# Two heads' value products as one piece of half-width matmuls, in a decoder layer on one Trainium2 core

## The chip, the core and the metric

The kernel runs on one core of a Trainium2 chip. Its engines run in parallel, each through its own queue in order: TensorE (PE for its matmuls, PEld for the loads of the stationary operand), VectorE (DVE), ScalarE (ACT), GpSimd (POOL) and SyncE (SP, which here issues the DMAs). The metric is the device time of one execution in microseconds (us). An execution that is profiled has a span, from the first to the last instruction, and a time of its own that is a little longer.

## The reference

The input is x, 512 tokens by 1024 channels in float32. After an RMS norm one projection gives queries, keys, values and gates for two mixers.

- Mixer A (MoBA) has 8 heads of 64 channels. With 512 tokens there are two blocks of 256 keys, and top-3 plus the own block selects all of them, so each head is causal attention over 512 keys with a T5 bias that depends on the distance.
- Mixer B (NSA) has 8 heads in two groups of four; a group shares its keys and values. It has three branches: attention to 31 compressed positions, attention to selected blocks (all 8 of them here), and a window of 512 (everything before the query). The selected branch and the window branch are again causal attention over 512 keys, with keys and values of their own. The three are summed with sigmoid gates.

Both outputs y are multiplied by SiLU(z), go through their branch weights, are merged with sigmoid gates, and pass the output projection, whose result is added to x. For this change the core is, for each head:

```
P = softmax(scale * Q K^T + bias, causal)      512 x 512
O = P V                                        512 x 64
y = O * SiLU(z)
```

MoBA has 8 such products, NSA 16 (8 heads by 2 branches), and NSA adds the compressed branch to the same sum.

## The kernel before

**Numbers in two parts.** All matmuls work on operands split into a high and a low part, hi + lo. The projections use a float32 form in three passes (hi·hi, hi·lo, lo·hi). P and V are split into float16 hi and lo.

**Units.** A `Unit` is one attention product: 8 for MoBA, 16 for NSA. For query block b (128 queries, b from 3 down to 0), `Unit.qk` makes the scores of b+1 key blocks in PSUM. `Unit.bias` (DVE, line 1117) adds the bias table T, takes the row minimum and writes a score buffer of the tag "sb" (7 of 3 KB a partition). `Unit.soft` computes exp (ACT, L1128), the gate factor and reciprocal, P's high part (ACT, L1135) and its low part (DVE, L1139), both float16, into the same buffer. `Unit.send` has SP issue one DMA transpose (L243) that writes P's 2(b+1) blocks, turned, into the unit's tile "dst", and the score buffer is free when it has landed. There are two dst tiles; `Unit.start` takes one when there is room.

**Value products.** `Unit.pv(kb)` (L1152) multiplies for key block kb, in the order 0, 3, 2, 1. The stationary operand is the 128 x 128 tile [V_hi | V_lo] of that key block, the moving operand P's turned blocks, 512 - 128 kb columns, first the high and then the low part: 8 matmuls for a unit, with 512, 512, 128, 128, 256, 256, 384 and 384 columns. PSUM tile O (one buffer of one bank) collects V_hi·P in rows 0 to 63 and V_lo·P in rows 64 to 127. A MoBA unit fills O alone; in NSA the two branches of a head add up in one O, and `before` (L1291) adds the compressed branch with one 128 x 128 matmul of 512 columns (`vz`, V of that branch, with rows of the other head set to zero).

**Taking O out.** `o_out` adds the two halves for each of the 16 heads: ACT copies rows 64 to 127 out with a scale (L1179), and DVE computes rows 0 to 63 times the scale plus that copy (L1183) into rows of `ys`, a tile of a pair of heads. When the second head is there and the gate `zs` is ready, `y_try` multiplies y by z (L1193), and ACT and DVE split it into hi and lo (L1194, L1195).

**Order.** The order of all instructions is made when the program is built: a small planner runs streams (`Run`) against planned costs of each engine and of the DMA queue. Stream A issues scores, V the value products, Z takes dst tiles, F the large projections, B and Y prepare; `yield n` gives a piece its planned cost, and a piece is issued when the planner holds its inputs for ready. F fills TensorE while attention waits. F's last part, `branch(1, j)` and the output, needs all y of mixer B. On the chip each engine then runs its list in order, with semaphores.

**Other buffers.** "nxn" is the scratch of the QK norms (two buffers; ACT writes squares at L772, DVE sums them at L773), "a" a pool of 27 tiles of 2 KB, "ge" four small tiles.

Of the kernel before, what the change touches and what calls it, by code (L numbers as in the profile page):

```python
# [12 lines left out]
F32 = mybir.dt.float32  # L13
# [16 lines left out]
C32 = 32  # L30
CMPH = 256
# [10 lines left out]
NATT = 27  # L42
NQK = 6
NSB = 7
NXN = 2
# [61 lines left out]
def hybrid_kernel(ctx: ExitStack, tc: tile.TileContext, x, x0, xT, wtok, wchan, gains, w1,  # L107
# [28 lines left out]
    RES = {"g": (pg, 2), "s": (pss, 2), "t": (pst, 3), "o": (pso, 1), "sb": (sp, NSB), "gmt": (sp, 3), "nraw": (sp, 4),  # L136
# [319 lines left out]
    first = alloc("dst", "x0", (P, 2048))  # L456
# [358 lines left out]
    def proj_norm(name, first=False, tags="gggg"):  # L815
        two = []

        def emit(t, ps):
# [7 lines left out]
            if name == "kb":  # L826
                e_ = sp.tile([P, 24], F32, name=nm("ge"), tag="ge", bufs=4)
                ch.do({"A": 164}, lambda e: e.activation(e_, ps[:, 256:280], AF.Exp, scale=nrx[:, t:t + 1]))
# [173 lines left out]
    def compress_v2(G):  # L1002
# [12 lines left out]
        vt = att("vz").rearrange("p (g i d) -> p g i d", g=2, i=2)  # L1015
# [23 lines left out]
    class Unit:  # L1039


        def __init__(u, q, ks, v, T, gate, first, last, before=None, after=None):
            u.q, u.ks, u.v, u.T, u.gate = q, ks, v, T, gate
            u.first, u.last, u.before, u.after = first, last, before, after
            u.c = {}
            u.st = u.mate = u.dst = None
            u.early = False
            u.todo = []

# [4 lines left out]

        def start(u):
            yield lambda: 0.0 if u.todo else None
            yield room("dst")
            u.dst = alloc("dst", "dst", (P, 2 * NT * S), F16)
            for f in u.todo:
                f()  # L1060

        def send(u, b, z):
# [6 lines left out]
            t = dma_transpose(u.blocks(b * P, n, S), z["pp"], n)  # L1069
# [3 lines left out]
        def blocks(u, o, n, step):  # L1073
            a = u.dst[:, o:o + P]
            return bass.AP(tensor=a.tensor, offset=a.offset, ap=[list(a.ap[0]), [step, n], [1, P]])

        def moving(u, kb, i):
            step = P + i * S
            return u.blocks(kb * step + (i + kb) * S, NT - kb, step)
# [30 lines left out]
        def bias(u, c, b, sps, frees, T, last=False):  # L1110
            z, L, st = {}, P * (b + 1), u.stats()

            def f(e):
                z["t"] = alloc("sb", "sb", (P, 3 * S // 2))
# [6 lines left out]
            c.do({"D": 57 + cd(L)}, f, frees, "sb")  # L1121
# [22 lines left out]
        def pv(u, kb):  # L1144
            yield need(*(("p", id(u), b) for b in range(kb, NT)))
            if kb == 0 and u.first:
                yield room("o")
                O[0] = psum("o", "O")
            n, v = S - kb * P, u.v()[kb]
            out = O[0][:, S - n:].rearrange("p (b q) -> p b q", q=P)  # L1150
            for i in range(2):
                nc.tensor.matmul(out, v, u.moving(kb, i), start=(u.first and kb == i == 0),  # L1152
                                 stop=(u.last and kb == i == 1 and not u.before))
            yield 2 * max(3 + 0.417 * n, 70)
            if kb == 1:
                release(u.dst)
            if kb == 1 and u.last:
                if u.before:
                    yield from u.before(O[0])
                u.after(O[0])  # L1160
# [6 lines left out]
    def o_out(O, m, h):  # L1167
        k = (m, h // 2)
        row = 64 * (h % 2)
        if row == 0:  # L1170
            ys[k] = att("ys", F32)
        y = ys[k]
        ch = Chain(now[0] + 230)
        z = {}
        r = vst[:, int(m == "b"), KT + 3:KT + 4]

        def f(e):
            z["t"] = alloc("gmt", "ot", (DH, S))
            e.activation(z["t"], O[64:128, :], AF.Copy, scale=r[64:128])  # L1179
        ch.do({"A": 571}, f, None, "gmt")  # L1180

        def f(e):
            e.scalar_tensor_tensor(y[row:row + 64, :], O[0:64, :], r[0:64], z["t"], op0=ALU.mult, op1=ALU.add)  # L1183
            release(O, ch.t)
        ch.do({"D": 659}, f, lambda: z["t"])
        if row:
            ch.mark(("ys",) + k).call(lambda: y_try(k))

    def y_try(k):
        if ("ys",) + k in done and ("zs",) + k in done:  # L1190
            y, z, hi, lo = ys[k], zs[k], att("yh"), att("yl")
            ch = Chain(max(done[("ys",) + k], done[("zs",) + k]))
            ch.do(either(512), lambda e: e.tensor_mul(y, y, z))  # L1193
            ch.do({"A": ca(512)}, lambda e: e.copy(hi, y))  # L1194
            ch.do(either(512), lambda e: e.tensor_sub(lo, y, hi.bitcast(F32)))  # L1195
            ch.mark(("y",) + k)
            yhl[k] = hi, lo, ch


    def moba_units():  # L1200
        us = []
        for h in range(8):
# [4 lines left out]
            def pre(h=h, p=p, i=i, box=box):  # L1207
                if i == 0:
# [6 lines left out]
                     lambda h=h: heads("v", h), lambda box=box, i=i: box["T", i], None, True, True, None, lambda o, h=h: o_out(o, "a", h))  # L1215
            us.append((pre, u))
        return us


    def nsa_units(g):  # L1220
# [63 lines left out]
        for i in range(4):  # L1284
            h = 4 * g + i
            for br in range(2):
                def before(o, i=i):
                    yield lambda: 0.0 if len(box["c"]) > i // 2 else None
# [441 lines left out]
```

## Time and profile before

| | |
|---|---|
| time, three runs | 426.15 to 426.85 us, median 426.71 |
| profiled execution | 427.12 us, span 424.9 us, granted clock 1.00 |
| PE busy, PEld busy | 415.7 us (98%), 325.9 us (77%) |
| DVE busy, ACT busy | 366.1 us (86%), 307.3 us (72%) |
| value products (L1152) | 192 matmuls, first at 71.1 us, last at 318.2 us |
| mean share of the DMA queue's packets | 69.7% of 16 engines' span |

A busy PE is not a PE at its peak: matmuls overlap in the pipeline, and a matmul's row shows its latency, not the time until the next may start. How fast PE goes is read from the starts of matmuls that follow one another.

### The profile page before, as it was taken

The page shows a single profiled execution, that of the slowest core. Times are in us where ns is not written, and L with a number is a line of the kernel's source. Part 1 is how long each engine was busy: PE and PEld are TensorE (multiplying, and loading weights), DVE is VectorE, ACT ScalarE, POOL GpSimd, SP SyncE. Part 2 cuts the span into 40 slices and gives each one's busy share as a digit, 9 for nine tenths or more (in the row PEclk, how much of TensorE's full clock was granted, in tenths as well). Part 3 has the DMA queues.
Part 4 walks back from the last instruction along what each step waited for, and adds up shares of the span by engine and source line. Part 5 has one row for each costly group of instructions (what it writes and reads, how often), then busy time and mean ns, then how long its engine had stood idle before and what let it go on. Part 6 is the DMA issues. An engine that isn't in the chain of part 4 may idle for free.

```text
span 424.9 us, 7105 instructions
## 1 busy us (share of the span) xinstructions
PE 415.7 (98%) x2131; PEld 325.9 (77%) x2131; DVE 366.1 (86%) x946; ACT 307.3 (72%) x809; POOL 36.4 (9%) x37
## 2 busy tenths in 40 slices
PE   9999999999998999999999999999999999999996
PEld 8878876778976777987777766666678888888886
DVE  6968779999899898969999998997966876699993
ACT  7997658897799799728999998897953543445620
POOL 0016000125220214000000000000000000000000
PEclk9999999999999999999999999999999999999999
DMA  8961967668989988821879679779878499170233
GB/s 290 298 201 37 184 215 177 131 166 208 261 238 216 196 157 201 225 88 25 165 154 174 169 187 183 166 127 198 150 183 305 144 383 322 43 222 3 61 137 100
DMA packets 116693, 75.30 MB, mean 177 GB/s; under 512 B 89072, under 2 KB 92016, under 8 KB 116656
## 3 DMA queue, kind: packets, MB, share of 16 engines
q1 hardware_dynamic: 116656, 74.86, 69.7%
q8 instruction: 17, 0.28, 0.3%
q14 instruction: 20, 0.16, 0.2%
HBM read 51.11 MB, written 2.75 MB: 127 GB/s over the span
## 4 chain that ended last, share of the span: by engine, by line
PE 55%; ACT 19%; DVE 14%; DMA 5%; issue 5%; SPq 0%; POOL 0%; DVEq 0%; ACTq 0%; POOLq 0%
PE pgc L435 17%; PE pgt L435 12%; PE po L435 9%; PE pbr L435 6%; DMA dst<-sb 5%; PE pgf L697 5%; ACT sb L1128 5%; ACT wh L400 4%; ACT sb L1135 3%; DVE sb L1117 3%; DVE sb L1139 3%; DVE wl L410 2%; PE O L1152 2%; PE sps L1097 1%; ACT vh L400 1%
## 5 line engine op out<-in xcount | busy, mean ns | idle before, releaser
L435 PE MATMUL pgc<-hh,wh 128*128 128x512 f32 x208 | 86.8, 417 | 0.0
L435 PE MATMUL pgc<-hh,wl 128*128 128x512 f32 x208 | 81.5, 392 | 0.0
L435 PE MATMUL pgc<-hl,wh 128*128 128x512 f32 x208 | 81.3, 391 | 0.0
L410 DVE TENSOR_TENSOR wl<-wr,wh 128x512 fp32r<-128x512 f32 (+1 forms) x112 | 73.3, 667 | 9.2 <-ACT wh L400 8.8
L400 ACT CAST wh<-wr 128x512 fp32r<-128x512 f32 (+1 forms) x111 | 64.1, 598 | 8.7 <-DMA wr<-in_wbr 5.2
L1128 ACT ACTIVATE sb<-sb,sst 128x512 f32<-128x512 f32 (+3 forms) x96 | 53.1, 554 | 14.0 <-DVE sst L1117 13.7
L435 PE MATMUL pgt<-wh,hh 128*128 128x512 f32 (+2 forms) x160 | 58.6, 366 | 0.1
L435 PE MATMUL pgt<-wl,hh 128*128 128x512 f32 (+2 forms) x160 | 56.0, 350 | 0.8 <-DVE wl L410 0.8
L435 PE MATMUL pgt<-wh,hl 128*128 128x512 f32 (+2 forms) x160 | 55.9, 349 | 0.0
L1117 DVE CUSTOM_DVE_ANT_0 sb<-sps,T,gst 128x512 f32<-128x512 f32 (+3 forms) x96 | 51.4, 545 | 5.1 <-DMA dst<-sb 3.5
L1139 DVE SCALAR_TENSOR_TENSOR sb<-sb,sst 128x512 f16<-128x512 f32 (+3 forms) x96 | 51.0, 547 | 3.2 <-ACT sb L1135 2.8
L1135 ACT ACTIVATE sb<-sb,sst 128x512 f16<-128x512 f32 (+3 forms) x96 | 50.6, 551 | 3.4 <-DVE sst L1131 3.0
L435 PEld LDWEIGHTS pgc<-hh,wh 128*128 128x128 f32 x208 | 39.2, 188 | 8.6
L435 PEld LDWEIGHTS pgc<-hh,wl 128*128 128x128 f32 x208 | 39.1, 188 | 8.5
L435 PEld LDWEIGHTS pgc<-hl,wh 128*128 128x128 f32 x208 | 39.2, 188 | 6.8
L487 POOL TENSOR_TENSOR nr<-nss,mhalf 128x8 f32<-128x8 f32 (+1 forms) x16 | 30.9, 1937 | 108.1 <-DVE nss L486 80.5
L1097 PE MATMUL sps<-qkt,qkt 128*128 128x384 f16 (+3 forms) x160 | 36.0, 319 | 1.8 <-DVE sst L1117 1.7
L435 PEld LDWEIGHTS pgt<-wl,hh 128*128 128x128 f32 x160 | 30.2, 189 | 5.2 <-DVE wl L410 1.4
L435 PEld LDWEIGHTS pgt<-wh,hh 128*128 128x128 f32 x160 | 30.2, 189 | 4.5 <-DVE X L910 0.4
L435 PEld LDWEIGHTS pgt<-wh,hl 128*128 128x128 f32 x160 | 30.2, 189 | 3.2
L435 PE MATMUL pbr<-yh,wh 128*128 128x512 f32 x64 | 26.5, 414 | 0.0
L1097 PEld LDWEIGHTS <-qkt 128*128 128x128 f16 x160 | 11.1, 98 | 19.2 <-issue 14.4
(229 smaller groups left out, 781.9 us busy)
## 6 DMA issues: line engine op xcount, KB each, us to landing
wr<-in_wchan SPq DMA_DIRECT2D x52, 256.0 KB, 3.4
wr<-in_wtok SPq DMA_DIRECT2D x36, 256.0 KB, 3.8
wq<-in_wout SPq DMA_DIRECT2D x36, 256.0 KB, 4.7
T<-rtab SPq DMA_DIRECT2D x16, 256.0 KB, 4.0
wr<-in_w SPq DMA_DIRECT2D x16, 256.0 KB, 3.2
wr<-in_wbr SPq DMA_DIRECT2D x16, 256.0 KB, 3.5
xr<-in_x SPq DMA_DIRECT2D x8, 256.0 KB, 5.4
x<-in_xT SPq DMA_DIRECT2D x7, 256.0 KB, 5.5
```

What stands on the lines that cost most here:

```text
L400: e.copy(hi, raw)
L410: c.do(either(n), lambda e, hi=hi, lo=lo, raw=raw: e.tensor_sub(lo, raw, hi.bitcast(F32))).mark((w, 1, i))
L435: nc.tensor.matmul(dst, sts[i][a], mvs[i][b], start=(start and i == a == b == 0), stop=(stop and i == n - 1 and (a, b) == passes[-1]), ski ...
L487: c.do({"p": 700 + 150 * w}, lambda e: e.tensor_tensor(v(dst), v(ss), mhalf[:parts, :w], op=ALU.pow))
L697: nc.tensor.matmul(ps[t][:, :n], (hl if a else hh)[:, k, t * P:(t + 1) * P], ws[k][b], start=(k == a == b == 0), stop=(k == KT - 1 and b = ...
L1097: nc.tensor.matmul(sps[:, :n].rearrange("p (t n) -> p t n", n=P), qs, k4[:, x, j, :b + 1], start=not x, stop=bool(x))
L1117: e.tensor_tensor_reduce(z["sb"], sps[:, :L], T[:, S - L:], scale=nrunscale, scalar=3e38, op0=ALU.add, op1=ALU.min, accum_out=st[:, 0, b:b ...
L1128: c.do({"A": 279 + 0.834 * L}, lambda e: e.activation(z["sb"], z["sb"], AF.Exp, bias=st[:, 0, b:b + 1], scale=-1.0, accum_out=st[:, 1, b:b ...
L1135: e.activation(z["pp"][:, :L], z["sb"], AF.Copy, scale=s_)
L1139: c.do({"d": 59 + cd(L)}, lambda e: e.scalar_tensor_tensor(z["pp"][:, L:], z["sb"], s_, z["pp"][:, :L], op0=ALU.mult, op1=ALU.subtract))
L1152: nc.tensor.matmul(out, v, u.moving(kb, i), start=(u.first and kb == i == 0), stop=(u.last and kb == i == 1 and not u.before))
```

## The change

`Pair` takes the value products of two units, in MoBA of two neighbouring heads, in NSA of one branch of two neighbouring heads (two pairs add up in one O). A half-width matmul has a stationary operand of 64 columns, V_hi or V_lo of one unit, and writes 64 rows of O: the first unit rows 0 to 63, the second rows 64 to 127. For each key block there are three products, V_hi·P_hi, V_lo·P_hi and V_hi·P_lo, each for the first and then the second unit: 24 matmuls for a pair, issued as one piece with a planned cost. V_lo·P_lo is left out. All eight parts of P must have landed before the first matmul.

O now holds two heads' finished sums, so `o_out` runs once for a pair: with `zs` ready one DVE operation of 128 x 512 computes O times the scale times z; otherwise ACT copies O with the scale into `ys` and DVE multiplies by z later. The compressed branch takes two 128 x 128 matmuls for a pair of heads (V_hi, V_lo) in place of one for each head.

The dst tile holds 40 blocks of 128 columns (10 KB a partition in place of 8), the second unit's blocks laid between the first's (`row`), so that each transpose writes one unbroken stretch. There are still two dst tiles, now of a pair each. Score buffers become 5 large ("sb", b = 3, 2) and 4 of half the size ("sh", b = 1, 0). To make room, "nxn" has one buffer, the pool "a" 26, "ge" three. The tiles that bring x for the last sum are taken from "dst" one at a time. The order of NSA's units becomes head 0 selected, head 1 selected, head 1 window, head 0 window.

```diff
-NATT = 27
+NATT = 26
-NSB = 7
-NXN = 2
+NSB = 5
+NSH = 4
+NXN = 1
...
-                vz[g], vh[:, g].rearrange("p s d -> p (s d)").bitcast(F32).unsqueeze(1).to_broadcast([P, 2, P]),
-                hmask.unsqueeze(2).to_broadcast([P, 2, P])), vh if g else None)
+                vz[g], vh[:, g].bitcast(F32).unsqueeze(2).to_broadcast([P, 2, 2, DH]),
+                hmask.unsqueeze(1).unsqueeze(3).to_broadcast([P, 2, 2, DH])), vh if g else None)
...
-            t = dma_transpose(u.blocks(b * P, n, S), z["pp"], n)
+            o = u.row(b)
+            t = dma_transpose(u.dst[:, o * P:(o + n) * P].rearrange("p (n q) -> p n q", q=P), z["pp"], n)
...
+        def row(u, b):
+            return 38 - 12 * b if u.side else 10 * b
...
-            z, L, st = {}, P * (b + 1), u.stats()
+            z, L, st, tag = {}, P * (b + 1), u.stats(), "sb" if b > 1 else "sh"
...
-        def pv(u, kb):
-            yield need(*(("p", id(u), b) for b in range(kb, NT)))
...
-            for i in range(2):
-                nc.tensor.matmul(out, v, u.moving(kb, i), start=(u.first and kb == i == 0),
-                                 stop=(u.last and kb == i == 1 and not u.before))
-            yield 2 * max(3 + 0.417 * n, 70)
...
+        def pv(p):
+            yield need(*(("p", id(u), b) for u in p.us for b in range(NT)))
...
+            for kb in (0, 3, 2, 1):
+                n = S - kb * P
+                for vi, pi in ((0, 0), (1, 0), (0, 1)):
+                    for r, u in enumerate(p.us):
+                        out = o[DH * r:DH * r + DH, S - n:].rearrange("p (b q) -> p b q", q=P)
+                        nc.tensor.matmul(out, v[r][kb][:, vi * DH:(vi + 1) * DH], u.moving(kb, pi),
+                                         start=p.first and kb == vi == pi == 0,
+                                         stop=p.last and kb == pi == 1 and not p.before)
+            yield 200 + sum(3 * 0.417 * (S - kb * P) for kb in range(NT))
+            release(p.dst)
...
-        def f(e):
-            z["t"] = alloc("gmt", "ot", (DH, S))
-            e.activation(z["t"], O[64:128, :], AF.Copy, scale=r[64:128])
-        ch.do({"A": 571}, f, None, "gmt")
...
-            e.scalar_tensor_tensor(y[row:row + 64, :], O[0:64, :], r[0:64], z["t"], op0=ALU.mult, op1=ALU.add)
...
+        if ("zs",) + k in done:
+            z = zs[k]
+            ch.t = max(ch.t, done[("zs",) + k])
+            ch.do({"D": 602}, lambda e: e.scalar_tensor_tensor(z, O, r, z, op0=ALU.mult, op1=ALU.mult), O)
+            y_split(k, ch)
+        else:
+            y = ys[k] = att("ys", F32)
+            ch.do({"A": 571}, lambda e: e.activation(y, O, AF.Copy, scale=r), O)
...
-                    nc.tensor.matmul(o, vz[g][:, i % 2, :], ch, start=False, stop=True)
-                    yield cm(S)
+                for z in range(2):
+                    nc.tensor.matmul(o, vz[g][:, z].rearrange("p i d -> p (i d)"), ch, start=False, stop=bool(z))
+                yield 2 * cm(S)
```

More of the change, by code (lines that the diff above doesn't have):

```diff
@@ L455, in hybrid_kernel @@
     now[0] = 700.0
-    first = alloc("dst", "x0", (P, 2048))
+    first = alloc("dst", "x0", (P, NBLK * P // 2))
     xat = {}
@@ L1039, in hybrid_kernel, with __init__ @@
     class Unit:
-        def __init__(u, q, ks, v, T, gate, first, last, before=None, after=None):
-            u.q, u.ks, u.v, u.T, u.gate = q, ks, v, T, gate
-            u.first, u.last, u.before, u.after = first, last, before, after
+        def __init__(u, q, ks, v, T, gate, last):
+            u.q, u.ks, u.v, u.T, u.gate, u.last = q, ks, v, T, gate, last
             u.c = {}
@@ L1048, in __init__ @@
             u.todo = []
+            u.side = 0
         def stats(u):
@@ L1142, in soft, with __init__, start @@
             return c
-        def pv(u, kb):
-            yield need(*(("p", id(u), b) for b in range(kb, NT)))
-            if kb == 0 and u.first:
+    class Pair:
+        def __init__(p, us, first, last, before, after):
+            p.us, p.first, p.last, p.before, p.after = us, first, last, before, after
+            us[1].side = 1
+        def start(p):
+            yield lambda: 0.0 if any(u.todo for u in p.us) else None
+            yield room("dst")
+            p.dst = alloc("dst", "dst", (P, NBLK * P), F16)
+            for u in p.us:
+                u.dst = p.dst
+                for f in u.todo:
+                    f()
+        def pv(p):
+            yield need(*(("p", id(u), b) for u in p.us for b in range(NT)))
+            if p.first:
                 yield room("o")
                 O[0] = psum("o", "O")
-            n, v = S - kb * P, u.v()[kb]
-            out = O[0][:, S - n:].rearrange("p (b q) -> p b q", q=P)
-            for i in range(2):
-                nc.tensor.matmul(out, v, u.moving(kb, i), start=(u.first and kb == i == 0),
-                                 stop=(u.last and kb == i == 1 and not u.before))
-            yield 2 * max(3 + 0.417 * n, 70)
[L1155 to L1160, printed above, removed]
+            o, v = O[0], [u.v() for u in p.us]
+            for kb in (0, 3, 2, 1):
[8 more added lines that the diff above has]
+            release(p.dst)
+            if p.last:
+                if p.before:
+                    yield from p.before(o)
+                p.after(o)
     O = [None]
@@ L1214, in moba_units @@
             u = Unit((n, 0, h % 4), (n, 1 + h % 4 // 2, i),
-                     lambda h=h: heads("v", h), lambda box=box, i=i: box["T", i], None, True, True, None, lambda o, h=h: o_out(o, "a", h))
+                     lambda h=h: heads("v", h), lambda box=box, i=i: box["T", i], None, True)
             us.append((pre, u))
+            if i:
+                pairs.append(Pair([z for _, z in us[-2:]], True, True, None, lambda o, p=p: o_out(o, ("a", p))))
         return us
@@ L1282, in pre1, with before @@
                     e, ch, pt.bitcast(F32)), pt)))
[L1284 to L1288, printed above, removed]
[L1289 to L1292 removed]
+        for j in range(2):
+            def before(o, j=j):
+                yield lambda: 0.0 if len(box["c"]) > j else None
+                ch, c = box["c"][j]
+                yield c.ready
+                for z in range(2):
+                    nc.tensor.matmul(o, vz[g][:, z].rearrange("p i d -> p (i d)"), ch, start=False, stop=bool(z))
+                yield 2 * cm(S)
+            duo = []
+            for i, br in ((0, 0), (1, 0), (1, 1), (0, 1)):
+                i += 2 * j
+                h = 4 * g + i
                 def pre(i=i, h=h, br=br):
@@ L1310, in hybrid_kernel @@
     sides = []
+    pairs = []
     units = moba_units() + nsa_units(0) + nsa_units(1)
@@ L1328, in starts @@
     def starts():
-        for _, u in units:
-            yield from u.start()
+        for p in pairs:
+            yield from p.start()
     def values():
-        for _, u in units:
-            for kb in (0, 3, 2, 1):
-                yield from u.pv(kb)
-            todo_units[0] -= 1
+        for p in pairs:
+            yield from p.pv()
+            todo_units[0] -= 2
     def zgate(m, j):
```

79 lines of the change are left out of this document (32 added, 47 removed).

## The prediction

> **What bounds the kernel now.** I read the busy shares first, then the stretches, then the chain of waits in order of time, then single pieces on TensorE.
>
> ```profile
> span 424.9 us, 7105 instructions
> PE 415.7 (98%) x2131; PEld 325.9 (77%) x2131; DVE 366.1 (86%) x946; ACT 307.3 (72%) x809; POOL 36.4 (9%) x37
> ```
> ```profile
> 20.00:40.00 20.00, 20.00 (x92) 16.21 (x92) 14.73 (x39) 16.71 (x40) 7.28 (x9) 1.00 0.42 135
> 40.00:60.00 20.00, 20.00 (x91) 16.17 (x90) 14.92 (x38) 11.51 (x33) 2.07 (x5) 1.00 0.92 208
> ...
> 60.00:110.00 50.00, 49.05 (x265) 38.17 (x264) 48.67 (x137) 42.93 (x128) 10.13 (x5) 1.00 0.70 172
> 110.00:170.00 60.00, 58.39 (x318) 44.88 (x317) 56.30 (x170) 54.76 (x162) 14.41 (x9) 1.00 0.92 204
> 170.00:205.00 35.00, 34.73 (x235) 29.39 (x234) 30.29 (x83) 22.49 (x61) 0.91 (x2) 1.00 0.45 119
> 205.00:260.00 55.00, 54.38 (x290) 38.76 (x290) 52.92 (x164) 50.74 (x145) 0.00 (x0) 1.00 0.83 166
> 260.00:320.00 60.00, 58.36 (x294) 41.56 (x293) 50.45 (x147) 49.67 (x138) 0.00 (x0) 1.00 0.79 171
> 320.00:394.00 74.00, 74.00 (x328) 61.30 (x327) 58.83 (x105) 32.69 (x63) 0.00 (x0) 1.00 0.59 201
> ```
>
> The columns of a stretch are its length, then busy time of PE, PEld, DVE, ACT and POOL, the granted clock, the DMA share and GB/s. TensorE at full clock (1.00) is the bound: from 320 to 394 us it is never idle. Attention runs from 60 to 320 us. There PE is idle for 0.95 + 1.61 + 0.27 + 0.62 + 1.64 = 5.09 us, and DVE is busy for 48.67 + 56.30 + 30.29 + 52.92 + 50.45 = 238.6 of 260 us. So a change can pay in two ways: fewer microseconds of TensorE work, or a lighter DVE and ACT that let TensorE idle less. What it takes off DVE does not count by itself.
>
> **TensorE's share of the change.** Chain of waits in order of time (start, length, what):
>
> ```profile
> 297.94 1.10 PE O L1152 x8
> 299.04 1.39 PE pgc L435 x6
> ...
> 318.78 4.79 PE pgc L435 x21
> 323.56 2.72 PE pbr L435 x12
> ```
>
> A unit's eight value matmuls take 1.10 us, 2 x (512+128+256+384) = 2560 columns, 0.43 ns a column, and the next work follows at once. 24 units cost 26.4 us, which is all that can be gained or lost at this place. A pair after the change has 24 matmuls and 3 x 2 x 1280 = 7680 columns, against 5120 for two units now: half as many again. What that costs depends on whether the two half-width matmuls of a step, which write rows 0 to 63 and rows 64 to 127, run at the same time. If they do, the pair streams 3840 columns, 1.65 us; if they don't, 7680 columns, 3.30 us. No row of this trace shows two narrow matmuls in different halves. The nearest are the four narrow ones of the compressed keys, here from TensorE's timeline and that of its loads:
>
> ```profile
> 140.10 0.40 PE L435 MATMUL pgt<-wl,hh 128*128 128x512 f32 x1
> 140.43 0.45 PE L975 MATMUL pk<-cst,gt 128*64 128x64 f32 x4
> 140.81 0.39 PE L1097 MATMUL sps<-qkt,qkt 128*128 128x256 f16 x2
> ```
> ```profile
> 140.43 0.31 PEld L975 LDWEIGHTS pk<-cst,gt 128*64 128x64 f32 x4 [0.36 <-DVE zs L1350]
> 140.80 0.11 PEld L1097 LDWEIGHTS <-qkt 128*128 128x128 f16 x2
> ```
> ```profile
> L975 PEld LDWEIGHTS pk<-cst,gt x4: 133/137/139, 140.4 to 140.6; 128*64 128x64 f32 x4
> L975 PE MATMUL pk<-cst,gt x4: 220/222/270, 140.4 to 140.7; 128*64 128x64 f32 x4
> ```
>
> Four loads of 64 columns start within 0.31 us less the last one's 0.137, so one every 0.058 us, with a matmul beside each: loads of half the width hide behind matmuls. And the work around them does not join: the following load starts at 140.80, though the last narrow matmul began near 140.43 + 0.45 - 0.22 = 140.66 and streams 64 columns (0.03 us), a hole of 0.11 us. A matmul on 64 rows shows the same:
>
> ```profile
> 25.54 0.84 PE L697 MATMUL pgf<-wh,hh 128*128 128x512 f32 x3
> 26.31 0.50 PE L872 MATMUL pR<-oh,rel 64*128 64x512 f32 x1
> ```
>
> Three matmuls of 0.227 us (1.39 us for six, above) from 25.54 end at 26.22, and the small one starts 0.09 us later. [...] I take the overlap, and keep 3.30 us for the rivals and for the range's top.
>
> The loads bound it from the other side. A step has two, so if they come one behind the other a step lasts at least 0.116 us. Only the three steps of 128 columns (0.055 us) are shorter: + 3 x 0.061 = 0.18 us, 1.83 us a pair. If the halves load together it stays 1.65. I take the middle, 1.74. [...]
>
> Each pair enters and leaves the narrow form once: 0.09 us of empty array and 0.06 for the first load on the way in; 0.09 to 0.11 and a load of up to 0.11 (a float32 one, which can't start early) on the way out: 0.36 us. In all 2.10 us a pair, 12 x 2.10 = 25.2 us, against 26.4: **-1.2 us**. Ends of this term with overlap: 12 x 2.00 - 26.4 = -2.4 (loads together), 12 x 2.24 - 26.4 = +0.5 (loads in line, and 0.05 for the second half to finish).
>
> The compressed branch stays at eight matmuls of the same size (two for each of four pairs, one for each of eight heads today): 0.
>
> **DVE's and ACT's share.**
>
> ```profile
> L1179 ACT ACTIVATE ot<-O,vst x16: 683/685/691, 74.4 to 318.8; 64x512 f32<-64x512 f32 x16
> L1183 DVE SCALAR_TENSOR_TENSOR ys<-O,vst,ot x16: 725/744/747, 77.2 to 319.5; 64x512 f32<-64x512 f32 x16
> ...
> L1193 DVE TENSOR_TENSOR ys<-ys,zs x8: 684/688/693, 105.9 to 320.3; 128x512 f32<-128x512 f32 x8
> ...
> L1379 DVE SCALAR_TENSOR_TENSOR gm<-gm,pbr x16: 664/682/689, 231.1 to 395.0; 128x512 f32<-128x512 f32 x16
> ```
>
> DVE spends 16 x 0.744 + 8 x 0.688 = 17.4 us on taking O out and the gate. Afterwards one operation of 128 x 512 per pair does it, on either path; a DVE pass over a PSUM tile of that size (gm at L1379) takes 0.68 us, so 8 x 0.69 = 5.5: 11.9 us less. ACT loses 16 x 0.685 = 11.0 and gets back up to 8 x 0.69 where the gate is not ready. 11.9 us is 5% of DVE's 238.6 us of attention. What of it reaches the end? At most PE's idle 5.09 us, at least nothing. These are its idle rows (us in all, times, longest), and one of DVE's:
>
> ```profile
> PE sps L1097 <- DVE sst L1117: 1.7, 3, 0.8
> PE O L1152 <- DMA dst<-sb: 0.9, 2, 0.7
> PE pgt L435 <- DVE wl L410: 0.8, 1, 0.8
> PE O L1152 <- DVE ys L1183: 0.6, 1, 0.6
> ```
> ```profile
> DVE sb L1117 <- DMA dst<-sb: 3.5, 5, 1.4
> ```
>
> DVE ends most of PE's (1.7, 0.8, 0.6). The last, O not yet read out, goes wholly. The others are spikes where DVE lags behind the planned order, and a lag shrinks with the load but doesn't vanish. I take half of the 5.09: **-2.5 us** (0 to -5.1). Two finer gains sit in that bound: nine score buffers and two dst tiles of a pair each ease the wait of DVE for a landed transpose (3.5 us, five times, L1117), and the transposes themselves stay 96, one SP issue each.
>
> **What is costed at nothing.** The single "nxn" tile: at the first norms four chains come at once.
>
> ```profile
> 34.74 0.69 DVE L773 TENSOR_REDUCE nss<-nxn 128x8 f32<-128x512 f32 x1
> ```
> ```profile
> 34.08 1.23 ACT L772 ACTIVATE nxn<-nraw 128x512 f32<-128x512 f32 x2 [0.23 <-DVE nss L773]
> ```
>
> With one buffer each later square waits for the sum before it, 3 x 0.68 = 2.0 us of ACT. ACT has 3.3 us free from 20 to 40 and 8.5 us from 40 to 60, so weight splits catch up; 2 us if they don't. Other norms come from gemm pieces some 5 us apart. Waiting for all eight parts of P makes a pair's product later than its first unit's today, but nothing behind it on PE is held while F has gates to compute. At the end that cover is thin:
>
> ```profile
> 317.30 1.25 PE L1152 MATMUL O<-dst,vb 128*128 128x512 f16 x8 [0.18 <-DMA dst<-sb]
> ```
>
> O's last matmuls begin at 317.30, and the last gate covers PE until 323.56. The new path from O to y is shorter by one ACT copy and one DVE pass (0.685 + 0.744 us) and longer by the second unit's product (about 1 us): even. "sb" at 5 holds back the output weights' loads a little in the last stretch (0 to 0.5 us). Pool "a" at 26 loses a tile but needs no `ys` where the gate is ready.
>
> **The sum.** Profiled execution 427.12 (span 424.9) - 1.2 - 2.5 = 423.4. The median of the runs, 426.71, is 0.4 below that execution, so **423.0**; its own range is 420 to 425.8.
>
> **The rivals.**
>
> *No overlap (slower).* The second half-width matmul waits for the first one's stream, in all 144 steps. Price: 12 x (3.30 + 0.36) = 43.9 us against 26.4, +17.5, less 2.5: 442.1, on the median's scale 441.7, range 436 to 444. It decides from 2.41 us a pair on, where (12 x 2.41 - 26.4) uses up the 2.5. [...] It is also the case in which the change does not do what its order of matmuls is laid out for.
>
> *One load in each step shows.* If the second half's matmul can start only when its load, begun with the first's stream, is there, and the next step waits for both: 1.65 + 12 x 0.058 = 2.35, with 0.36 it is 2.71 us a pair, +6.1, less 2.5: 430.3, 427 to 432. For it: the first load after a change of shape isn't hidden in the rows above; against: the four narrow loads were. [...]
>
> *The gain is eaten.* Overlap works, a pair costs 2.2 as two units do, and the idle holes only move: 427.1 + 0, 426.7, range 425.5 to 428. For it: PE is 98% busy, so there is little to win; the order is made anew by planned costs, and holes come where plan and chip differ.
>
> *Everything pays.* Halves load together and all idle goes: -2.4 - 5.1 = -7.5, 419.2, range 417 to 420.
>
> **Chances.** Forecast 0.48, everything pays 0.08, gain eaten 0.17, a load in each step 0.10, no overlap 0.17. Faster by over 0.2% (below 425.86; a smaller difference can't be told from none here): 0.48 + 0.08 + 0.01 of the third case = 0.57. Within 0.2%: 0.11, all of the third. Slower: 0.05 + 0.10 + 0.17 = 0.32. The range leaves out the case without overlap and small tails: 418 to 432.
>
> **What would show it.** Starts of the 24 matmuls: a piece of 1.7 to 2.0 us from first to last means overlap, over 3 none, 2.4 a load in each step. Holes of about 0.1 us before and after each piece show the change of shape. L1179 with its 64-row copies and L1193 must be gone or turned into at most eight; DVE's busy time must fall by about 12 us, ACT's by 5 to 11. PE's idle between 60 and 320 us should be near 2.5 us. I am wrong if DVE falls by 12 and PE's idle doesn't, if the pieces last longer than 2.4 us, or if ACT's squares between 32 and 38 us leave PE waiting for weights.

## The result and the profile after

The changed kernel takes 421.78 us (median of four runs, 420.18 to 422.54), the kernel before, beside it, 426.57 us (426.15 to 426.85). The ratio is 0.988, with an interval of 0.985 to 0.991: faster by 4.8 us (3.7 to 6.2). The forecast was 423.0, its own range 420 to 425.8. The profiled execution of the changed kernel took 422.54 us, 4.6 less than the one before.

Page of the changed kernel, head and busy time:

```profile
span 420.5 us, 7307 instructions
PE 411.8 (98%) x2235; PEld 322.0 (77%) x2235; DVE 356.3 (85%) x933; ACT 297.9 (71%) x793; POOL 35.1 (8%) x37
```

Its stretches, with the same edges as before (length, busy time of PE, PEld, DVE, ACT and POOL, granted clock, DMA share, GB/s):

```profile
20.00:40.00 20.00, 19.90 (x91) 15.81 (x90) 12.83 (x32) 15.90 (x36) 6.17 (x9) 1.00 0.43 137
...
60.00:110.00 50.00, 48.28 (x280) 37.16 (x279) 48.09 (x145) 41.75 (x127) 10.09 (x6) 1.00 0.76 183
110.00:170.00 60.00, 57.75 (x337) 45.63 (x336) 53.97 (x158) 54.08 (x158) 11.46 (x7) 1.00 0.91 205
170.00:205.00 35.00, 34.83 (x236) 29.45 (x235) 29.60 (x85) 21.92 (x59) 2.57 (x2) 1.00 0.51 120
205.00:260.00 55.00, 54.71 (x318) 38.88 (x317) 52.06 (x164) 47.70 (x141) 0.00 (x0) 1.00 0.80 171
260.00:320.00 60.00, 60.00 (x358) 42.55 (x357) 47.64 (x143) 46.65 (x135) 0.00 (x0) 1.00 0.85 178
```

TensorE is still the bound, at full clock (1.00). From 60 to 320 us it is idle for 1.72 + 2.25 + 0.17 + 0.29 + 0.00 = 4.43 us, against 5.09 before. So the idle time has hardly fallen, though DVE is busy 9.8 us less over the whole span and ACT 9.4 us less. Nearly all of the gain must be TensorE work that is no longer there. One pair on TensorE's timeline, and the chain of waits around the end of attention (start, length, what):

```profile
84.20 0.39 PE L437 MATMUL pgt<-wl,hh 128*128 128x512 f32 x1
84.52 1.82 PE L1168 MATMUL O<-dst,v 128*64 128x512 f16 x24
86.27 0.28 PE L1094 MATMUL sps<-qkt,qkt 128*128 128x128 f16 x2
```
```profile
316.50 1.75 PE O L1168 x24
318.25 0.66 PE O L1304 x2
318.92 2.96 PE pbr L437 x12
321.88 5.45 PE pgc L437 x24
```

The float32 matmul ahead of the piece ends its stream at 84.20 + 0.23 = 84.43, and the next full-width matmul starts at 86.27: a pair costs 1.84 us with both changes of shape, where two units cost 2.20. Ten of the twelve pieces take the same 1.75 or 1.76 us from their start to the next matmul. For 12 pairs that is 22.1 us against 26.4, 4.3 us less.

The chain also says where the gain appears. The value products of the last pair end at 318.25 here and the last unit's, before, between 318 and 319. Attention doesn't end sooner. But what TensorE has left after it is shorter: from 318.92 to the span's end at 420.5 are 101.6 us, and before, from 318.78 to 424.9, 106.1 us. The 4.5 us that the pairs left free inside attention were filled with projection pieces: up to 394 us and behind it TensorE has 327 + 114 matmuls from 320 us on, and in the kernel before 328 + 134.

Taking O out, as groups by tile (lowest, median and highest ns of one; first and last start):

```profile
L1190 DVE SCALAR_TENSOR_TENSOR zs<-O,vst,zs x5: 732/744/750, 150.4 to 319.0; 128x512 f32<-128x512 f32 x5
L1194 ACT ACTIVATE ys<-O,vst x3: 677/681/689, 86.4 to 167.7; 128x512 f32<-128x512 f32 x3
...
L1208 DVE TENSOR_TENSOR zs<-ys,zs x3: 682/682/684, 104.6 to 176.3; 128x512 f32<-128x512 f32 x3
```

Five of the eight pairs of heads find the gate ready. On DVE 5 x 0.744 + 3 x 0.682 = 5.8 us stand where 17.4 stood, on ACT 3 x 0.681 = 2.0 where 11.0 stood.

### The profile page after: what moved, and what is told of

The parts are those of the page before. It is cut to its first block, busy times and chain, and to the rows that moved or that the text cites. A ratio compares the mean times of both kernels' runs of the same rounds, so it can differ in the third digit from the quotient of the medians.

```text
span 420.5 us, 7307 instructions
## 1 busy us (share of the span) xinstructions
PE 411.8 (98%) x2235; PEld 322.0 (77%) x2235; DVE 356.3 (85%) x933; ACT 297.9 (71%) x793; POOL 35.1 (8%) x37
## 4 chain that ended last, share of the span: by engine, by line
PE 54%; DVE 23%; DMA 9%; ACT 5%; issue 5%; SPq 1%; POOL 1%; DVEq 0%; ACTq 0%; POOLq 0%
PE pgc L437 21%; PE pbr L437 9%; PE po L437 9%; PE pgt L437 8%; DMA wr<-in_wtok 5%; DVE sb L1114 4%; DVE wl L412 4%; DVE sb L1136 4%; DMA wr<-in_w 3%; PE O L1168 3%; PE sps L1094 3%; ACT wh L402 2%; DVE vl L412 1%; SPq L238 1%; DMA T<-rtab 1%
## 5 line engine op out<-in xcount | busy, mean ns | idle before, releaser
L412 DVE TENSOR_TENSOR wl<-wr,wh 128x512 fp32r<-128x512 f32 (+1 forms) x112 | 73.1, 669 | 11.8 <-ACT wh L402 11.6
L1125 ACT ACTIVATE sb<-sb,sst 128x256 f32<-128x256 f32 (+3 forms) x96 | 53.2, 554 | 10.5 <-DVE sst L1114 10.2
L1136 DVE SCALAR_TENSOR_TENSOR sb<-sb,sst 128x256 f16<-128x256 f32 (+3 forms) x96 | 51.1, 542 | 4.2 <-ACT sb L1132 3.9
L1114 DVE CUSTOM_DVE_ANT_0 sb<-sps,T,gst 128x512 f32<-128x512 f32 (+3 forms) x96 | 51.2, 541 | 3.5 <-PE sps L1094 1.6
L1132 ACT ACTIVATE sb<-sb,sst 128x256 f16<-128x256 f32 (+3 forms) x96 | 51.4, 552 | 4.0 <-DVE sst L1128 3.7
L1094 PE MATMUL sps<-qkt,qkt 128*128 128x512 f16 (+3 forms) x176 | 38.2, 310 | 1.6 <-DVE sst L1114 1.4
L489 POOL TENSOR_TENSOR nr<-nss,mhalf 128x8 f32<-128x8 f32 (+1 forms) x16 | 29.0, 1819 | 109.4 <-DVE nss L488 47.9
L437 PE MATMUL pbr<-yh,wh 128*128 128x512 f32 x64 | 26.4, 413 | 0.0
```

Source lines behind the costliest of these rows:

```text
L412: c.do(either(n), lambda e, hi=hi, lo=lo, raw=raw: e.tensor_sub(lo, raw, hi.bitcast(F32))).mark((w, 1, i))
L437: nc.tensor.matmul(dst, sts[i][a], mvs[i][b], start=(start and i == a == b == 0), stop=(stop and i == n - 1 and (a, b) == passes[-1]), ski ...
L489: c.do({"p": 700 + 150 * w}, lambda e: e.tensor_tensor(v(dst), v(ss), mhalf[:parts, :w], op=ALU.pow))
L1094: nc.tensor.matmul(sps[:, :n].rearrange("p (t n) -> p t n", n=P), qs, k4[:, x, j, :b + 1], start=not x, stop=bool(x))
L1114: e.tensor_tensor_reduce(z["sb"], sps[:, :L], T[:, S - L:], scale=nrunscale, scalar=3e38, op0=ALU.add, op1=ALU.min, accum_out=st[:, 0, b:b ...
L1125: c.do({"A": 279 + 0.834 * L}, lambda e: e.activation(z["sb"], z["sb"], AF.Exp, bias=st[:, 0, b:b + 1], scale=-1.0, accum_out=st[:, 1, b:b ...
```

## The experiments

Each kernel is the changed one with the edit shown, unless it says "before". Ratios are to the kernel before on the same chip. Where two kernels ran on different chips, their difference is that of their ratios times 426.6 us.

### Do the two halves work at the same time?

**All but one matmul of the second unit into the first half.**

```diff
-                        out = o[DH * r:DH * r + DH, S - n:].rearrange("p (b q) -> p b q", q=P)
+                        h = r if kb == vi == pi == 0 else 0
+                        out = o[DH * h:DH * h + DH, S - n:].rearrange("p (b q) -> p b q", q=P)
...
```

The second head's sum lands in the first one's rows, so its own rows lack it.

> The changed kernel with the second unit's half-width matmuls, but for the first, written into the first unit's half: the same 24 matmuls and loads, but two halves can't work side by side. The second head's sum lands in the first one's rows, so it is left out of its own. Theory (the pair's 1.66 us is overlap of the two halves): the stream grows to 1.66 + 1.28 + 0.16 = about 3.1 us a pair, +17 us, 438 to 440. Rival (half-width matmuls run at twice the rate each): 422.

Measured: 436.99 us, ratio 1.024 (1.022 to 1.026), 15 us over the changed kernel, a little under what the theory said. TensorE's timeline of this kernel:

```profile
84.25 3.23 PE L1169 MATMUL O<-dst,v 128*64 128x512 f16 x24
87.42 0.28 PE L1094 MATMUL sps<-qkt,qkt 128*128 128x128 f16 x2
```

From the piece's start to the next full-width matmul it is 3.17 us, against 1.75 in the changed kernel. The same 24 loads and 24 streams cost 1.4 us a pair more when they share a half; 12 x 1.42 = 17 of TensorE, 15 at the end. Without the overlap the change would be a loss: the ratio here is 1.024.

**Order within the piece: three matmuls of the first unit, then three of the second, for each key block.**

```diff
-                for vi, pi in ((0, 0), (1, 0), (0, 1)):
-                    for r, u in enumerate(p.us):
+                for r, u in enumerate(p.us):
+                    for vi, pi in ((0, 0), (1, 0), (0, 1)):
```

> The changed kernel with the two loops of a key block swapped: the three products of the first unit, then the three of the second, so that neighbours in the queue write the same half. Nothing else moves, the planned cost included. Theory (TensorE's stream sets the end, and all that the pair saves there is overlap of neighbours): within a key block only the turn from one unit to the next can overlap, so a pair's stream goes from 1.66 us to between 2.8 and 3.3, and the time goes up by 12 x 1.1 to 1.65, 13 to 20 us, to 435 to 442. Rival (half-width matmuls are cheap by themselves, order does not matter): 422. Rival (TensorE has slack in attention): up by less than 8 us.

Measured: 421.88 us, ratio 0.988 (0.985 to 0.991), the same as the changed kernel. I had expected that TensorE starts matmuls in the order given, so that three in one half would be followed by three in the other. TensorE's timeline, first whole, then for the 0.04 us from 84.16:

```profile
84.16 1.83 PE L1168 MATMUL O<-dst,v 128*64 128x512 f16 x24
85.92 0.28 PE L1094 MATMUL sps<-qkt,qkt 128*128 128x128 f16 x2
...
84.16 0.41 PE L1168 MATMUL O<-dst,v 128*64 128x512 f16 x2
```

Two matmuls begin within 0.04 us of each other. The trace doesn't name their halves, but in the next run, whose first nine are all of one half, only one begins in the first 0.07 us. So I read the second here as the second unit's first, fourth in the program's order, begun ahead of two matmuls of the first unit. From the piece's start to the next full-width matmul it is 1.76 us. The theory falls.

**All twelve of the first unit, then all twelve of the second.**

```diff
-            for kb in (0, 3, 2, 1):
-                n = S - kb * P
-                for vi, pi in ((0, 0), (1, 0), (0, 1)):
-                    for r, u in enumerate(p.us):
+            for r, u in enumerate(p.us):
+                for kb in (0, 3, 2, 1):
+                    n = S - kb * P
+                    for vi, pi in ((0, 0), (1, 0), (0, 1)):
```

> The changed kernel with all twelve matmuls of the first unit issued before the twelve of the second. In the run with three and three the two halves started within 0.01 us of each other, so the queue looks past a matmul whose half is busy. Theory A (it looks far enough, 24 matmuls and loads): 421 to 423. Theory B (it looks only a few ahead): the second unit starts late, 1 to 1.6 us a pair, 434 to 441.

Measured: 432.05 us, ratio 1.013 (1.011 to 1.014), 10 us over the changed kernel. Its timeline, and the group of the matmuls that begin between 84.00 and 85.09 us:

```profile
84.03 2.88 PE L1168 MATMUL O<-dst,v 128*64 128x512 f16 x24
86.84 0.29 PE L1094 MATMUL sps<-qkt,qkt 128*128 128x128 f16 x2
```
```profile
L1168 PE MATMUL O<-dst,v x9: 219/272/403, 84.0 to 85.1; 128*64 128x512 f16 x3, 128*64 128x128 f16 x3, 128*64 128x256 f16 x3
```

2.81 us to the next full-width matmul: part of the overlap is there, and the time lies between the two theories. The first nine matmuls to begin are all the first unit's, since no more than three have 512 columns; the second unit's first begins at 85.09, 1.06 us after the piece's start, when three of the first unit have yet to begin. So in this order too it began ahead of some of the first unit's, but of three only; the written order of the change needs none of this.

### What does a pair cost?

**V_lo·P_lo put back**, 32 half-width matmuls a pair.

```diff
-                for vi, pi in ((0, 0), (1, 0), (0, 1)):
+                for vi, pi in ((0, 0), (1, 0), (0, 1), (1, 1)):
...
```

> The changed kernel with the fourth product V_lo P_lo put back as half-width matmuls: 32 instead of 24 for a pair, 5120 columns of overlapped stream, as many as two units of the kernel before. Theory (overlap gives nothing by itself, what is saved is the left-out product): +0.55 us a pair, +6.6 us, 428.4, so slower than the kernel before by the change of shape (12 x 0.2) less what else the change brings: 426 to 429. Rival (the gain lies in pairing, buffers or order): +2 us or less.

Measured: 426.59 us over ten runs, ratio 0.9995 (0.998 to 1.001): the time of before. A pair on its timeline, and its stretches:

```profile
84.56 2.36 PE L1168 MATMUL O<-dst,v 128*64 128x512 f16 x32
86.86 0.29 PE L1094 MATMUL sps<-qkt,qkt 128*128 128x128 f16 x2
```

```profile
60.00:110.00 50.00, 48.21 (x287) 36.72 (x286) 48.15 (x145) 41.65 (x126) 9.03 (x6) 1.00 0.80 192
110.00:170.00 60.00, 59.15 (x358) 46.91 (x358) 53.62 (x158) 53.66 (x159) 9.30 (x7) 1.00 0.90 198
170.00:205.00 35.00, 34.97 (x237) 29.67 (x236) 29.53 (x83) 21.86 (x59) 2.57 (x2) 1.00 0.54 125
205.00:260.00 55.00, 54.99 (x337) 38.63 (x336) 51.99 (x163) 48.07 (x142) 0.00 (x0) 1.00 0.79 167
260.00:320.00 60.00, 60.00 (x364) 42.77 (x362) 47.64 (x141) 46.84 (x134) 0.00 (x0) 1.00 0.80 171
```

The fourth product makes a piece 2.30 us long in place of 1.75: 1280 columns a half cost 0.55 us, so the 3840 of the changed kernel's pair stream for 1.65. This is the change with the streams of before: half-width work, lighter DVE and ACT, but four products. PE is idle for 1.79 + 0.85 + 0.03 + 0.01 = 2.68 us, 2.4 less than before, and the time is the same. As it looks in this one profile, what relief brought, the changes of shape took. The gain of the whole change is about as large as what leaving the product out brings (4.7 us). Half the width is what allows that: the full-width tile [V_hi | V_lo] multiplies P_lo by both.

**Three more changes of shape in a pair**: after each of the first three key blocks one full-width matmul of 64 columns, with zeros in both operands.

```diff
+                if kb != 1:
+                    nc.tensor.matmul(o[:, S - P:S - DH], warm[:, :1].to_broadcast([P, P]),
+                                     warm[:, :1].to_broadcast([P, DH]), start=False, stop=False)
```

> The changed kernel with a full-width matmul of 64 columns (zeros, added to O) after each of the first three key blocks of a pair: 36 more changes of array shape there and back, everything else in place. Theory (each way costs 0.09 us of empty array and a first load of 0.03): 0.24 to 0.30 us each with its own stream of 0.03, +8.6 to +10.8 us, 430 to 433. Rival (changing shape costs nothing, the holes seen are the semaphores'): 36 x 0.03 to 0.06, +1 to +2 us, 423 to 424.

Measured: 429.45 us, ratio 1.005 (1.003 to 1.007), 7.2 us over the changed kernel for 36 insertions: 0.20 us each, less than the theory's 0.24 to 0.30, in which the 64 columns stream for 0.03. Its timeline:

```profile
85.16 0.84 PE L1168 MATMUL O<-dst,v 128*64 128x512 f16 x6
85.93 0.20 PE L1172 MATMUL O<-warm 128*128 128x64 bf16 x1
86.06 0.36 PE L1168 MATMUL O<-dst,v 128*64 128x128 f16 x6
```

Six matmuls of 512 columns, two at a time, stream 0.66 us and end near 85.82; the full-width one starts 0.11 us later, and the next narrow ones 0.13 us after that. A pair that starts narrow and ends full-width once should then pay about 0.2 us, and it does: 1.84 - 1.65 = 0.19, with the stream from the run with four products.

### What does the lighter VectorE and ScalarE bring?

**The old way of taking O out put back**, with nothing told to the planner: two ACT copies and two DVE passes of 64 x 512 for a pair, and DVE's product with z.

```diff
+    def old_sum(s, O, r):
+        for h in (slice(0, DH), slice(DH, P)):
+            nc.scalar.activation(s[h, :], O[h, :], AF.Copy, scale=r[h])
+            nc.vector.scalar_tensor_tensor(s[h, :], O[h, :], 0.0, s[h, :], op0=ALU.mult, op1=ALU.add)
...
```

> The changed kernel with the old work of taking O out put back without the planner knowing: for each pair two ACT copies and two DVE passes of 64 x 512 and a DVE product with the gate, at the places where the changed kernel has one operation, so that every queue keeps its order. DVE gets some 11.6 us more, ACT some 8.9. Theory A (the gain is TensorE's streams alone, DVE's relief is off the path): 0 to +1 us, 422 to 423. Theory B (as predicted, half of the gain or more is the relief): +2.5 us or more, 424.3 to 427.

Measured: 444.43 us, ratio 1.041 (1.038 to 1.043), 22 us over the changed kernel and far beyond what either theory allowed. The waits of its engines:

```profile
DVE ys L1186 <- ACT ys L1185: 17.4, 14, 6.2
```

Beside the load there is a new wait: 14 of the 16 DVE passes wait for ACT's copy, and DVE is idle meanwhile, for 17.4 us in all and 6.2 at the longest. The granted clock is lower as well, 0.94 from 110 to 170 us and 0.97 from 205 to 260, where the changed kernel has 1.00. This is no measure of load alone.

**The split of y done three times**, again not told to the planner; no operation waits for one that wasn't there before.

```diff
-        ch.do({"A": ca(512)}, lambda e: e.copy(hi, y))
-        ch.do(either(512), lambda e: e.tensor_sub(lo, y, hi.bitcast(F32)))
+        ch.do({"A": ca(512)}, lambda e: [e.copy(hi, y) for _ in range(3)])
+        ch.do(either(512), lambda e: [e.tensor_sub(lo, y, hi.bitcast(F32)) for _ in range(3)])
```

> The changed kernel with load that brings no new wait: where a pair's y is split, ACT makes its copy three times and DVE its difference three times, to the same tiles, in the same places of the same queues, unknown to the planner. That adds 16 x 0.62 = 9.9 us to ACT and 16 x 0.69 = 11.0 us to DVE, about what the change took off them (9.4 and 9.8 by the busy times). Theory A (DVE's and ACT's relief is off the path): 0 to +1.5 us, 422 to 423.5. Theory B (as predicted): at least +2.5, 424.3 or more. If it goes far beyond, as when the old sums went back in unplanned (444.4), even pure load in a planned queue is dear.

Measured: 431.81 us, ratio 1.013 (1.010 to 1.016), 10 us over the changed kernel, for 9.9 us more of ACT and 11.0 more of DVE. The theory that DVE's and ACT's load is off the path allowed 1.5 us. It falls.

**The order alone, and the order with the load.** The first kernel tells the planner that DVE's difference takes 1.38 us longer for each pair of heads, and does not do it. The second is told the same and does the difference three times; its instructions stand in the same order.

```diff
...
-        ch.do(either(512), lambda e: e.tensor_sub(lo, y, hi.bitcast(F32)))
+        ch.do({"d": cd(512) + 1380}, lambda e: e.tensor_sub(lo, y, hi.bitcast(F32)))
```
```diff
...
-        ch.do(either(512), lambda e: e.tensor_sub(lo, y, hi.bitcast(F32)))
+        ch.do({"d": cd(512) + 1380}, lambda e: [e.tensor_sub(lo, y, hi.bitcast(F32)) for _ in range(3)])
```

> The changed kernel with only the planner told that each pair's difference y - hi takes 1.38 us longer on DVE (8 x 1.38 = 11.0 us in all); nothing is done there. The order is one made for a heavier DVE, and it is run light. It is compared with the next run, which has the same order and does the work. Theory A (only unplanned load hurts; planned load and relief cost and bring next to nothing): this one within 1.5 us of the next, both 421 to 425. Theory B (DVE's load is worth its half or more): this one 5 us or more faster than the next.

> The same order as the run before, and DVE makes each pair's difference three times, 16 x 0.69 = 11.0 us more. Theory A: 421 to 425, and at least 6 us under the 431.8 of the run that did such work unplanned. Theory B: 427 or more.

Measured: 425.55 us, ratio 0.996 (0.994 to 0.997), and 433.59 us, ratio 1.014 (1.010 to 1.019). The first does the changed kernel's work, but for four operations (L1033) that went from DVE to ACT, and is 3 us slower (1.7 to 4.5): the order that the planner happens to make is worth that much. From the first to the second it is 8.0 us for 11.0 us of DVE work, with a wide spread: the second's four executions took 431.1 and 432.1 us at a granted clock of 1.00, and 435.1 and 435.5 at 0.996, so 5.6 to 9.9 us. TensorE's waits between 60 and 320 us, first without the load, then with it:

```profile
PE sps L1094 <- DVE sst L1114: 2.9, 3, 1.4
```
```profile
PE sps L1094 <- DVE sst L1114: 7.0, 8, 1.8
PE hps L940 <- DVE vl L412: 2.2, 4, 1.3
```

The scores' matmuls wait for a PSUM buffer that DVE has yet to read (L1114): three times without the load, eight times with it. The planner knew of this load, and still 0.5 to 0.9 us of each microsecond comes through, though TensorE is busy 98% of the time in the changed kernel. The second trace is of the execution of 435.1 us, in which the granted clock falls to 0.71 from 180 to 185 us, behind some of these waits; the quicker two may have waited less. DVE is a second bound inside attention.

**The kernel before, with only the lighter way of taking O out.**

```diff
...
-        row = 64 * (h % 2)
...
+        if h % 2 == 0:
+            Chain(now[0] + 230).do({"D": 70}, lambda e: e.tensor_copy(tiny, O[:, :1]), O)
+            return
...
```

> The kernel before with only the lighter way of taking O out: the second head of a pair is read as in the changed kernel (one operation of 128 x 512 with the gate, or an ACT copy), the first head's O is read in one column and dropped, so the sum of the halves and every first head are left out of the result. TensorE's work is that of before, DVE gets about 11 us lighter, ACT 5 to 11, and the planner knows. Theory A (relief off the path): 426 to 427.5. Theory B (half of TensorE's 5.1 us idle or more): 422 to 424.

Measured: 429.42 us over nine runs, ratio 1.006 (1.004 to 1.008): slower than before, with less work. Neither theory has that. In its stretch from 110 to 170 us TensorE is idle for 6.0 us, against 1.6 before, and its longest waits there are for transposes and for queries:

```profile
110.00:170.00 60.00, 53.98 (x290) 41.06 (x290) 50.35 (x159) 46.51 (x139) 12.98 (x8) 1.00 0.90 192
```
```profile
PE O L1153 <- DMA dst<-sb: 2.2, 2, 1.6
PE sps L1098 <- DMA qkt<-qk: 1.7, 1, 1.7
```

The planner, which knew of the lighter work, made another order, and that order's loss may cover what the relief gained; no run parts the two. What relief alone brings in an unchanged order stays open.

### The single scratch tile, and larger pieces

**The kernel before with one "nxn" tile.**

```diff
-NXN = 2
+NXN = 1
```

> The kernel before with one buffer for the norms' squares in place of two; every queue keeps its order. The prediction costed it at nothing, with 2 us as its bound. Theory: 426 to 427.2, since ACT has room from 32 to 60 us. Rival: up to +2 us, 428.6.

Measured: 428.59 us, ratio 1.003 (1.0007 to 1.005): 1.2 us slower (0.3 to 2.1). ACT's timeline of the changed kernel shows the wait that had been foreseen, squares about 1.4 us apart, each behind the sum of the one before:

```profile
33.00 0.65 ACT L774 ACTIVATE nxn<-nraw 128x512 f32<-128x512 f32 x1
34.40 0.63 ACT L774 ACTIVATE nxn<-nraw 128x512 f32<-128x512 f32 x1 [0.75 <-DVE nss L775]
35.78 0.63 ACT L774 ACTIVATE nxn<-nraw 128x512 f32<-128x512 f32 x1 [0.75 <-DVE nss L775]
```

But TensorE doesn't pay for it there. This is the stretch around it of the kernel before with one tile:

```profile
20.00:40.00 20.00, 20.00 (x93) 16.12 (x92) 12.90 (x33) 15.90 (x37) 6.39 (x9) 1.00 0.40 132
```

TensorE is busy for all of the 20 us. The execution with this profile is the quickest of the five (427.52 us), so the place where the others lose their microsecond was not seen.

**NSA's two pairs of one O in one piece of 48 matmuls**, which would save half of NSA's changes of shape.

```diff
+        def pv(p, lead=None):
+            ps = [lead, p] if lead else [p]
+            yield need(*(("p", id(u), b) for q in ps for u in q.us for b in range(NT)))
...
+            if p.last:
+                yield from p.pv(lead)
...
+            lead = None if p.last else p
```

> The changed kernel with NSA's two pairs of one O multiplied in one piece, 48 half-width matmuls, so that eight changes of shape remain of twelve. A change there and back cost 0.21 us in the run with 36 more of them: -0.9 us, 420.9, if nothing else gives. Against it: both dst tiles are held until the second pair has landed, so transposes of the next units start late; if TensorE runs out of other work by that, slower than 421.8.

Measured: 433.73 us, ratio 1.014 (1.013 to 1.016), 11 us over the changed kernel. TensorE's waits between 60 and 320 us:

```profile
PE O L1170 <- DMA dst<-sb: 7.1, 2, 6.2
```

The piece needs both dst tiles at once, so no transpose of the next pairs can land until it has run, and TensorE waits up to 6.2 us for them. Right behind 320 us it waits once more, and then works at half the clock. This is its timeline, and the stretch (with the granted clock, 0.50, third from the end):

```profile
325.27 3.48 PE L1170 MATMUL O<-dst,vb 128*64 128x512 f16 x24 [2.58 <-DMA dst<-sb]
328.68 0.80 PE L1306 MATMUL O<-ch,vz 128*128 128x512 f32 x1
```
```profile
325.00:330.00 5.00, 4.73 (x27) 3.46 (x27) 0.06 (x1) 0.00 (x0) 0.00 (x0) 0.50 0.87 302
```

These 24 matmuls take 3.41 us to the next full-width one, where they take 1.75 in the changed kernel. The clock is 0.50 from 317 us, in the midst of the longer wait, to 330. So the two waits, 6.2 and 2.6 us, are not the whole of the 11.

## Why the prediction came out

**The bound** was read rightly: TensorE, with nothing idle after 320 us before or after the change, so that only work taken from TensorE, or its idle time in attention, could count.

**The overlap** was the step with the most at stake. That two halves work at the same time was my assumption, which no row of before showed, and it held: 1.75 us for a pair's piece where 1.7 to 2.0 had been named as its sign, and 3.17 when the halves are made to coincide. The rivals "no overlap" (441.7) and "one load in each step shows" (430.3) fall with it; "everything pays" (419.2) falls by its time. The nearest row, four narrow loads hidden behind narrow matmuls, pointed the right way. A pair's 7680 columns stream in 1.65 us, against 3.30 one after another at the 0.43 ns a column of before: 2.0 times.

**TensorE's term was sized too small**: -1.2 us predicted, -4.3 measured in the profile, outside the term's ends of -2.4 to +0.5. Two parts of it failed. The change of shape had been put at 0.36 us a pair, with an empty array and a load on either side. That was my estimate, and no run shows the array empty or a load in the hole; measured, the way there and back is 0.19 to 0.20 us in all, and in the run with three more changes the next start comes 0.11 us after the stream's end on the way out and 0.13 us later on the way back. The way out is no dearer where the next full-width load is a float32 one, for which 0.11 us had been set aside; in the changed kernel it is 1.75 us there too:

```profile
100.40 1.82 PE L1168 MATMUL O<-dst,v 128*64 128x512 f16 x24
102.15 0.40 PE L437 MATMUL pgt<-wh,hh 128*128 128x280 f32 x1
```

And the stream had been put at 1.74, between loads that run together and loads in line; it is 1.65, the end at which the loads run together. TensorE's loads in the changed kernel, those that begin within 0.1 us at a pair's start, show it:

```profile
84.52 0.14 PEld L1168 LDWEIGHTS <-v 128*64 128x64 f16 x4 [0.35 <-issue]
```

Four half loads take 0.14 us in all, so the price of 0.058 us one after the other, taken from float32 rows, was too high for float16.

**DVE's and ACT's term was sized too large as it ended**: half of the idle time, -2.5 us, had been taken, and 2.5 us of idle time named as its sign; 5.09 us became 4.43, -0.7. In part that is the mechanism of the rival "the gain is eaten": the holes move. But with four products the idle time did fall by 2.4, to 2.68. And the run with the order by unit, whose work and time are the changed kernel's, is idle for 1.60 + 1.01 + 0.30 = 2.91 us in the stretches that aren't full:

```profile
60.00:110.00 50.00, 48.40 (x282) 37.58 (x281) 48.17 (x144) 42.65 (x129) 9.03 (x6) 1.00 0.79 191
110.00:170.00 60.00, 58.99 (x340) 46.35 (x339) 55.18 (x161) 54.73 (x161) 9.30 (x7) 1.00 0.91 209
...
205.00:260.00 55.00, 54.70 (x311) 38.76 (x309) 52.03 (x161) 48.04 (x141) 0.00 (x0) 1.00 0.81 175
```

That execution took 420.83 us, the profiled one of the changed kernel 422.54: two executions of the same work can differ by 1.5 us in idle time, and one profile can't size this term. The medians speak for "too large": TensorE's 4.3 us leave 0.5 of the gain of 4.8 (3.7 to 6.2), and leaving out the fourth product takes 6.6 us of stream but brings 4.7 (3.3 to 6.2). So the two terms do not seem to add. That a shorter piece brings TensorE's next work forward, where it meets DVE, ACT and the transposes sooner, would explain it; no run shows it. The whole as a budget, with one profile of each kernel: from before to four products, 12 x 0.2 for the changes of shape, less 2.4 of idle time, is 0, measured 0 (ratio 0.9995). From there to three products, 12 x 1280 columns x 0.43 ns = 6.6 us of stream less, 1.75 us of idle time more, is -4.8, and the ratios differ by 4.7 us. That order made anew has a share in each of these steps, up to the 3 us seen with the planner told otherwise, can't be excluded. So the forecast of -3.7 on the profile's scale, where -4.6 came, has the overlap right, but its sum is right in part by luck: one term was too small and the other too large.

**What was costed at nothing.** The single "nxn" tile costs 1.2 us when it alone is put into the kernel before, not nothing, within the 2 us named as the price of lost cover. The cover that was named, ACT's free time until 60 us, did hold in the profile; where the loss arises stays open. The two compressed matmuls, 0.66 us a pair, are the eight of before. Waiting for all eight parts of P was said to hold nothing up on TensorE; once it did:

```profile
146.67 0.40 PE L1168 MATMUL O<-dst,v 128*64 128x512 f16 x1
147.86 1.66 PE L1168 MATMUL O<-dst,v 128*64 128x512 f16 x22 [0.79 <-DMA dst<-sb]
```

The second unit's transpose was there 1.2 us after the first unit's first matmul had begun, and 0.8 us of TensorE was lost. At the end, where the cover looked thin, nothing was: from 260 to 320 us TensorE is busy for the whole 60.00 us. The score buffers' smaller number held nothing back in the last stretch.

**Load.** DVE fell by 9.8 us where 12 was said, ACT by 9.4, within 5 to 11. In the operations named, DVE lost 17.4 - 5.8 = 11.6; the rest is other work, which I did not sort.

## What to carry to other kernels

Try two products of half the array's width side by side, with results in different halves and matmuls that alternate: here a pair took 1.75 us so, 1.76 with three and three, 2.81 with twelve and twelve, and 3.17 in one half. Group many of them, since entering and leaving the narrow form cost about 0.2 us here. Where one engine is busy 98% of a stage and another 89%, as TensorE and DVE from 60 to 320 us here, don't count on the gains on the two to add: extra work on the second came through at 0.5 to 0.9 us for each microsecond. Before comparing small changes in a kernel whose order is planned, find out how much a new order alone moves the time; here it was 3 us, two thirds of the gain.

## What the hardware showed that I had not expected

With three matmuls of the first unit and then three of the second, two began within 0.04 us of each other, the second of them, as I read it, ahead of two earlier ones of the first unit. In the order unit after unit the second unit's first began 1.06 us after the first unit's, ahead of three, and the pair took 2.81 us in place of 1.75. So in these two runs TensorE's queue, described above as in order, did not start the matmuls of two halves in the program's order. A wait for a transpose went otherwise: the first unit's first matmul began at 146.67 us, and its 512 columns stream in 0.22 us at 0.43 ns each; that unit's next matmul takes the same columns of P, but nothing began until 147.86 us, when the transpose had landed for which the second unit's matmul, between the two, waited. A change from half to full width and back cost 0.20 us (36 of them, 7.2 us). And in the run with two pairs in a piece the granted clock fell to 0.50 at 317 us, during a wait of 6.2 us, and stayed there until 330 us; 24 matmuls took 3.41 us at that clock in place of 1.75. Whether the wait brought the clock down, no run here tests.
